# Column-grouped sums of squares, a table for low-rank products, a re-planned instruction order and a divided last multiply in a hybrid RWKV-7 / DeltaNet layer

## The chip, the cores and the metric

The kernel runs on one core of a Trainium2 chip. The metric is the device time of one execution in microseconds, as the median of several runs: 2253.88 us over 3 runs (2250.65 to 2256.99) before the change. The engines are named as in the profile: PE is TensorE, and PEld its weight loads, DVE is VectorE, ACT is ScalarE, POOL is GpSimd, SP is SyncE, which issues most of the DMAs.

## The reference

One layer over 256 latent tokens and 256 context tokens, width D = 2048, all in float32. Cut to what matters:

```python
mod = silu(c) @ w_ada + b_ada                      # six vectors of D: shifts, scales, gates
h  = rmsnorm(x, norm1_w)   * (1 + sc1)  + sh1      # and hc from ctx with its own vectors
rw, cv, z, ab, gt = split(h @ w_in)                # one input projection
o_a = two-way RWKV-7 scan over 16 heads of 64      # low-rank decay, rate and gate inputs
o_b = two-way chunked gated DeltaNet, 8 heads of 128
    # u = silu(conv(cv)); q, k = l2norm(q), l2norm(k); v
m = sigmoid(g_a) * (o_a @ p_a) + sigmoid(g_b) * (o_b @ p_b)
x = x + gt1 * (m @ w_out)
x = x + gt2 * (silu(h2 @ w_gate) * (h2 @ w_up)) @ w_down
return rmsnorm(x, final_norm_w)
```

`rmsnorm(x, w)` is `x * rsqrt(mean(x * x) + 1e-6) * w`. The context states start the latent scans; only the latent output is returned.

## The kernel before

Features lie on the 128 partitions (16 tiles of D), tokens along the free axis: 256 latent and 256 context columns, 512 together. Every large product splits both operands in a high and a low part, and sums three products (hi·hi, lo·hi, hi·lo); a weight tile is loaded (`wraw`), cast on ACT (`whi`) and subtracted on DVE (`wlo`).

The kernel has four stages.

**First part** (lines 412 to 530, in program order by hand). The squares of x and of the context (ACT and DVE, line 447 and 448, two buffers `sq`) are summed over partitions by a product with a 128x128 matrix of ones (line 449), one for each of 16 tiles, all into one PSUM tile. A logarithm and an exponential give `rs`, the reciprocal root (lines 452 and 453). Then eight parts run, each for two tiles of D. A part loads four weight tiles `aw` of 1 MB (six buffers) and makes the modulation rows with narrow products, four column groups of 32 at a time (`ada_part`, line 461; four visits c = 0 to 3). `rows_of` (line 464) copies the rows, turns them on PE (line 469), and computes the modulated, normalised activations `hxh` and `hxl` of the two tiles. `low_products` (line 499) then adds this part's share to six accumulators: four groups of low-rank columns and the first key and receptance tile, in PSUM tiles `pi`, `mm`, `s`, `s`, `mm`, `pa`. It is a generator: one step is one accumulator, six products. These steps belong to the part before, and line 520 lays them between the visits of the present part: none after visit 0, one after visit 1, two after 2, one after 3, and the two left between the turn of the rows and their use. `low_split` (line 486) casts the low-rank weights, behind whose buffers on SP stand the next part's loads (`load_low`, `load_ada`).

**Woven stage** (`Weave`, lines 180 to 282). Some 20 kinds of generators yield operations for PE, DVE, ACT and POOL. A planner with a cost for each operation takes, again and again, the operation that could start first; where several could start at the same moment, the lowest rank wins (`RANK`, plus 10 for each pair or head). The order that comes out is fixed, engine by engine. The projection products (`products`, `cast`) have rank 900, so they fill PE where nothing else is ready; a gate column group has no reader in this stage, and `GATES_A` and `GATES_B` say after which pair (0 to 7) or head (0 to 7) how many of 40 may come. First come 8 pairs of RWKV heads (`prepare`, `grams`, `inverse`, `values`, `scan`), after the low-rank outputs (`lowrank`, `lowrank_out`), which ACT makes and stores to DRAM with DMAs of its own queue; then 8 DeltaNet heads (`features`, `tokens`, `decays`, `head_grams`, `head_inverse`, `head_scan`). In `features` ACT runs a Silu over 1280 columns, then a table load is planned, and `l2n` squares k on ACT, sums over partitions on PE with the ones and goes on with a logarithm on ACT and a multiply on DVE. In the planner a DMA that is issued on ACT or DVE costs 0.06 us (line 125), and Silu costs its elements alone.

**Merge, output projection, FFN, down projection** (lines 1515 to 1685), ordered by the framework.

**End** (lines 1686 to 1689). After the last residual add the squares, summed on the way, are summed over partitions; ACT takes the logarithm and the exponential (`rms_scale`, line 388), and DVE multiplies the 16 tiles by the scale in five pieces, each followed by its store on SP.

Rows of the profile for the woven stage all carry line 147, where operations are recorded, so they are told apart by tile names: `arena` holds many of them, `lo` are the low-rank outputs, `pa`, `pi`, `s`, `mm` are PSUM tiles.

Of the kernel before, what the change touches and what calls it, by code (L numbers as in the profile page):

```python
# [13 lines left out]
AF = mybir.ActivationFunctionType  # L14
# [4 lines left out]
P = 128  # L19
D = 2048  # L20
KT = D // P
T = 256
# [2 lines left out]
NPAIR = 8  # L25
NGH = 8
DECAY = 0.6065306597126334
GATES_A, GATES_B = (6, 2, 3, 4, 0, 1, 4, 3), (2, 2, 0, 1, 0, 1, 10, 1)

RANK = dict(cast=-94, lowrank=-64, prepare=59, grams=-6, inverse=-56, values=6, scan=-39, begin=181, head_scan=145, head_inverse=100, head_grams=123, decays=122, tokens=77, features=120, gate_out=137, lowrank_out=105, row_tile=486)  # L30
LAT = dict(dma=2.04, hop=0.255, own=0.092, grp=32, cg=4, turn=0.17)
LNEXP = "natural_log_exp_and_others"
SIGM = "sigmoid_and_others"
# [79 lines left out]
class Lane:  # L113
# [5 lines left out]
    def __getattr__(self, name):  # L119

        def op(out, *a, **k):
            if name == "preload_act_table_set":
                return Op(self, 1.3, lambda: self.engine.preload_act_table_set(out))
            if name == "dma_start":
                return Op(self, 0.6 if self.each > 0.0012 else 0.06, lambda: self.engine.dma_start(out, *a))
            n = int(np.prod(out.shape[1:]))
            kind = "full"
            if name == "transpose" and len(a) == 2:
                cost = 0.109
            elif name == "matmul":  # L130
                rows, m = a[0].shape[0], out.shape[0]
                if a[0].dtype == F32R:
                    cost, kind = 0.0035 + 0.000448 * n, "split"
                elif rows <= 64 and m <= 64:
                    cost, kind = (0.01 + 0.00037 * n if rows < 64 else 0.01 + 0.00075 * n), (rows, m)
                elif m <= 64:
                    cost, kind = 0.058 if m == 64 else 0.14, (rows, m)
                else:
                    cost = (0.0054 + 0.00167 * n) * (1.22 if rows == 96 else 1)
            else:  # L140
                psum = a and getattr(a[0], "tensor", None) is not None and "PSum" in type(a[0].tensor).__name__
                cost = (self.psum if psum else self.fixed) + self.each * n
                if name == "tensor_tensor_scan":
                    cost *= 1.9
                elif name == "scalar_tensor_tensor" and not psum:
                    cost *= 1.2
            return Op(self, cost, lambda: getattr(self.engine, name)(out, *a, **k), kind)  # L147
        return op


def quad(ops):
# [127 lines left out]
def emit(ctx: ExitStack, tc, A, out, dbg=None):  # L279
    nc = tc.nc  # L280
    V, S, G, Q = nc.vector, nc.scalar, nc.gpsimd, nc.sync
    E = nc.tensor
# [3 lines left out]
    e, v, s = Lane(E, 0.0, 0.0, 0.0), Lane(V, 0.07, 0.00104, LAT["own"], 0.13), Lane(S, 0.09, 0.00086, LAT["own"], 0.165)  # L286
# [6 lines left out]
    pa = ent(tc.tile_pool(name="pa", bufs=2, space=PSUM))  # L293
    pi = ent(tc.tile_pool(name="pi", bufs=1, space=PSUM))
    psq = ent(tc.tile_pool(name="psq", bufs=2, space=PSUM))
# [16 lines left out]
    ident, ones, bd64 = c_("ident"), c_("ones"), c_("bd64")  # L312
# [6 lines left out]
    eps, gneps = c_("eps"), c_("gneps")  # L319
# [3 lines left out]
    def pst(pool, tag, shape=None):  # L323
        return pool.tile([P, 512], F32, tag=tag, name=tag)
# [60 lines left out]
    H2 = (hx.tile([P, KT, 2, T], F32R, name="hxh"), hx.tile([P, KT, 2, T], F32R, name="hxl"))  # L385
    HX = tuple(t.rearrange("p k a t -> p k (a t)") for t in H2)

    def rms_scale(pool, parts, n, name):

        ps = pst(pa, "pa")  # L390
        for i, sq in enumerate(parts):
            E.matmul(ps[:, :n], ones, sq, start=i == 0, stop=i == len(parts) - 1)
        r = pool.tile([P, n], F32, tag=name, name=name)
        S.activation(r, ps[:, :n], AF.Ln, bias=eps, scale=1.0 / D)
        S.activation(r, r, AF.Exp, scale=-0.5)
        return r

    def square_sum(pool, src, acc, first):

# [12 lines left out]
    with tc.tile_pool(name="p0", bufs=1) as p0, \  # L412
# [31 lines left out]
        ps = pst(pa, "pa")  # L444
        for k in range(KT):
            sq = p0.tile([P, 2, T], F32, tag="sq", name="sq", bufs=2)
            S.activation(sq[:, 0], xt[:, k, :], AF.Square)
            V.tensor_mul(sq[:, 1], ct[:, k, :], ct[:, k, :])
            E.matmul(ps, ones, sq.rearrange("p a t -> p (a t)"), start=k == 0, stop=k == KT - 1)
        rs = p0.tile([P, 2, T], F32, name="rs")  # L450
        S.preload_act_table_set(LNEXP)
        S.activation(rs.rearrange("p a t -> p (a t)"), ps, AF.Ln, bias=eps, scale=1.0 / D)
        S.activation(rs, rs, AF.Exp, scale=-0.5)
        s1 = p0.tile([P, 2, 16], F32, name="s1")

# [43 lines left out]
        def low_products(e, w):  # L499

            for ps, (o, m, n) in zip(low, LOWS):
# [2 lines left out]
                         e == 0 and k == 0, e == NE - 1 and k == 1)  # L504
                yield

        before = None
        for part in range(NE + 1):
            if part < NE:
                ps = pst(pmm, "mm")  # L510
            for c in range(4):
                if part + 1 < NE:
                    load_ada(part + 1, c)
                if part < NE:
                    ada_part(ps, part, c)
                if c == 0 and part < NE:
                    w = low_split(part)
                    if part + 1 < NE:
                        load_low(part + 1)
                for _ in itertools.islice(before or (), (0, 1, 2, 1)[c]):  # L520
                    pass
            if part < NE:
                rows_of(part, ps, before or ())
                before = low_products(part, w)
            else:
                for _ in before:
                    pass
# [162 lines left out]
    rs = rk_ctx.enter_context(tc.tile_pool(name="rs", bufs=1, reuse_waits="tile"))  # L690
# [5 lines left out]
    rs = Places(rs, arena, *rplaces)  # L696
# [30 lines left out]
    def lowrank():  # L727
# [17 lines left out]
        for p in range(NPAIR):  # L745
# [8 lines left out]
            for j in (0, 2, 1, 3):  # L754
                ps = yield psb
                yield e.matmul(ps, w[:96, 4 * (p % 2) + j], lin[:, j], start=True, stop=True)
                weave.add(RANK['lowrank_out'], lowrank_out(p, j, ps, out[j]))

    def prepare(p):
# [78 lines left out]
        if p + 1 < NPAIR:  # L838
            weave.add(10 * p + 10 + RANK['prepare'], prepare(p + 1))

# [222 lines left out]
    def products():  # L1063
# [24 lines left out]
        while todo or nxt:  # L1088
            if nxt is None:
# [4 lines left out]
                if nxt[0] == "g":  # L1094
                    nxt = "g", next(gate_next)
                weave.add(RANK['cast'], cast(source(*nxt), i))
            what, p = nxt
            nxt = choose()
            if nxt is not None:
                if nxt[0] == "g":  # L1100
                    nxt = "g", next(gate_next)
                weave.add(RANK['cast'], cast(source(*nxt), i + 1))
            ps = yield mmb
# [10 lines left out]
            if what == "g":  # L1114
                weave.add(RANK['gate_out'], gate_out(rs, p, ps))
            else:
# [127 lines left out]
    def features(h):  # L1244

        o = hd[h]
        yield ("scalars",)
        if h:
            yield "feat", h - 1
        if h > 1:  # L1250
            for n in ("tok", "gram"):
                yield n, h - 2
        kvq = gs.tile([P, 1280], F32, tag="kvq", name="kvq")
        o["k"], o["v"], o["q"] = k, vv, q = kvq[:, 0:512], kvq[:, 512:1024], kvq[:, 1024:1280]
        for what, j, t, n in (("K", 8 + h, k, 2), ("V", 16 + h, vv, 2), ("Q", h, q, 1)):
            yield what + "gemm", h
            yield from conv(o[what + "ps"], j, t, n)
        yield s.activation(kvq, kvq, AF.Silu)
        yield s.preload_act_table_set(LNEXP)
        yield from l2n(k, 512)  # L1260
        yield from l2n(q, T, float(P) ** -0.5)
        weave.ready("feat", h)
# [185 lines left out]
    def ada_rest():  # L1448
# [23 lines left out]
        for i in range(4 * KT):  # L1472
            if i > 2:
                yield "added", i - 3
            if i % 8 == 0 and i:
                yield "gscan", i // 8 - 1
            weave.add(RANK['row_tile'], row_tile(i))
            if i % KT == KT - 1:
# [85 lines left out]
    for j in range(KT):  # L1564
        if j == 8:
            wpool.append(more)
        ps = pst(pmm, "mm")
# [6 lines left out]
    x1p = Places(None, arena, ("x1", KT * T, 1), ("rs", T, 1), ("ssum", T, 1), ("graw", 64, 1), ("s2", 16, 1), ("pad", 176, 1),  # L1574
                 ("cb", 2048, 1), ("sq", T, 3), ("m", T, 2), ("hb", T, 2))
    x1 = x1p.tile([P, KT, T], F32, name="x1")
    ssum = x1p.tile([P, T], F32, name="ssum")
# [7 lines left out]
    for j in range(KT):  # L1585
        ps = pst(pmm, "mm")
# [13 lines left out]
    for j in range(KT):  # L1600
        ps = pst(pmm, "mm")
        gemm(ps[:, 0:T], load_w(A["wout"][j], P, KT), M, T)
        V.scalar_tensor_tensor(x1[:, j, :], ps[:, 0:T], mod[:, 32 + j:33 + j], x1[:, j, :], ALU.mult, ALU.add)
        sq = square_sum(x1p, x1[:, j, :], ssum, j == 0)
# [9 lines left out]
        elif j % 3 == 2 and j < 12:  # L1614
            hi, lo = (W4[:, i, j // 3] for i in range(2))
            for c in range(2):
                k, raw = slice(8 * c, 8 * c + 8), coming.pop(0)
# [3 lines left out]
    r = rms_scale(x1p, [ssum, sq], T, "rs")  # L1621
# [6 lines left out]
    with tc.tile_pool(name="fp", bufs=1, reuse_waits="tile") as fp:  # L1628
# [19 lines left out]
        for j in range(NH):  # L1648
            if j < 2:
                ps = p4[j]  # L1650
            else:
                ps = pst(pmm, "mm")
# [8 lines left out]
            if 2 <= j < 34:  # L1661

                for a in range(2):
                    c = (j - 2) // 2
# [10 lines left out]
        for j in range(KT):  # L1675
            ps = pst(pmm, "mm")
# [5 lines left out]
            sq = square_sum(x1p, x1[:, j, :], ssum, j == 0)  # L1682
            if 0 < j < KT - 1:
                V.tensor_add(ssum, ssum, sq)
            S.activation(x1[:, j, :], x1[:, j, :], AF.Identity, scale=p_("nf", j))
        r = rms_scale(x1p, [ssum, sq], T, "rs")
        for k0, k1 in ((0, 4), (4, 8), (8, 12), (12, 14), (14, 16)):
            V.tensor_mul(x1[:, k0:k1], x1[:, k0:k1], r.unsqueeze(1).to_broadcast([P, k1 - k0, T]))  # L1688
            Q.dma_start(out[:, k0:k1, :], x1[:, k0:k1, :])


# [94 lines left out]
```

## Time and profile before

| what | us |
|---|---|
| median of 3 runs | 2253.88 |
| the profiled execution | 2266.56 |
| its span, first to last instruction | 2264.7 |
| PE busy | 2166.1 |
| DVE busy | 1562.9 |
| ACT busy | 1063.7 |
| mean granted clock of PE | 0.982 |

A line of a profile that stands for a group of instructions gives line, engine, operation, what is written and what is read, the count, the busy time and the mean in ns, and then the idle time of the engine just before, with what ended it. In a timeline a row starts with its start and its length in us, and the idle time before it stands in brackets with what released it. A row of waits gives the waiting engine with its tile and line, who ended the wait, total us, times and the longest. A row of windows gives the stretch, its length, the busy time of PE, weight loads, DVE, ACT and POOL with their counts, the clock of PE that was granted (1.00 is full), the busy share of the DMA engines, and GB/s. The strip lines cut the span into 40 slices of about 57 us, with tenths as digits.

### The profile page before, as it was taken

To read this page: it belongs to the slowest core of one execution; us is meant where nothing else is said; L and a number is where in the kernel's file an instruction comes from. 1 tells how busy PE (TensorE), PEld (TensorE's weight loads), DVE (VectorE), ACT (ScalarE), POOL (GpSimd) and SP (SyncE) were. 2 spreads that over 40 slices of the span, in tenths; PEclk is the share of its full clock that TensorE was granted. 3 is DMA by queue.
4 is the path that set the end of the run, shared out by engine and by line. 5 is a ranking of instruction groups with operands and counts; after the bars stand their busy time and mean duration, and the time that the engine had idled before them with its cause. 6 is when DMAs were issued, how large, how long until landed. Compare 5 with 4: busy or idle time off the path is not lost. (4 is left out here: it accounts for less than half of the span.)

```text
span 2264.7 us, 54396 instructions
## 1 busy us (share of the span) xinstructions
PE 2166.1 (96%) x22778; PEld 1925.6 (85%) x22778; DVE 1562.9 (69%) x3253; ACT 1063.7 (47%) x1878; POOL 91.3 (4%) x169
## 2 busy tenths in 40 slices
PE   7998999999999999999999989999999999999998
PEld 4776588777778778877788989989999999999997
DVE  3456388778888668899898878865666665444544
ACT  3245555444554555454455554544444444444443
POOL 0000000000000010111110010000000000000000
PEclk9998999999999999999999999999999999999999
DMA  9955644344344346565558798845777776566665
GB/s 380 408 138 165 184 121 134 98 111 107 99 121 113 115 133 185 162 183 172 173 171 250 249 325 271 310 145 176 234 234 233 235 238 210 187 187 187 188 191 161
DMA packets 234485, 435.14 MB, mean 192 GB/s; under 512 B 115328, under 2 KB 129664, under 8 KB 229888
## 3 DMA queue, kind: packets, MB, share of 16 engines
q1 hardware_dynamic: 206304, 355.11, 50.5%
q0 software_dynamic: 14112, 51.39, 7.1%
q10 hardware_dynamic: 13824, 25.17, 3.3%
q8 instruction: 179, 2.93, 0.6%
q14 instruction: 66, 0.54, 0.1%
HBM read 405.76 MB, written 25.84 MB: 191 GB/s over the span
## 5 line engine op out<-in xcount | busy, mean ns | idle before, releaser
L364 DVE TENSOR_TENSOR wlo<-wraw,whi 128x1024 fp32r<-128x1024 f32 x328 | 392.7, 1198 | 331.6 <-ACT whi L363 329.3
L363 ACT CAST whi<-wraw 128x1024 fp32r<-128x1024 f32 x328 | 337.2, 1028 | 474.8 <-PE mm L374 377.4
L147 PE MATMUL mm<-hxh,whi 128*128 128x256 f32 (+1 forms) x1376 | 465.6, 338 | 7.7 <-ACT whi L147 7.5
L147 PE MATMUL mm<-hxh,wlo 128*128 128x256 f32 (+1 forms) x1376 | 466.5, 339 | 4.4 <-DVE wlo L147 4.3
L147 PE MATMUL mm<-hxl,whi 128*128 128x256 f32 (+1 forms) x1376 | 463.7, 337 | 0.0
L375 PE MATMUL mm<-hfh,wlo 128*128 128x256 f32 x1344 | 375.5, 279 | 0.4 <-DVE wlo L364 0.2
L374 PE MATMUL mm<-hfl,whi 128*128 128x256 f32 x1344 | 375.2, 279 | 0.0
L373 PE MATMUL mm<-hfh,whi 128*128 128x256 f32 x1344 | 375.2, 279 | 0.0
L147 PEld LDWEIGHTS mm<-hxh,whi 128*128 128x128 f32 x1376 | 265.0, 193 | 34.4 <-ACT whi L147 9.2
L147 PEld LDWEIGHTS mm<-hxh,wlo 128*128 128x128 f32 x1376 | 264.7, 192 | 30.9 <-DVE wlo L147 8.2
L147 PEld LDWEIGHTS mm<-hxl,whi 128*128 128x128 f32 x1376 | 264.7, 192 | 24.2 <-issue 3.0
L147 DVE TENSOR_TENSOR wlo<-wraw,whi 128x512 fp32r<-128x512 f32 x344 | 235.4, 686 | 68.4 <-ACT whi L147 65.5
L375 PEld LDWEIGHTS mm<-hfh,wlo 128*128 128x128 f32 x1344 | 252.7, 188 | 0.8 <-DVE wlo L364 0.8
L373 PEld LDWEIGHTS mm<-hfh,whi 128*128 128x128 f32 x1344 | 252.7, 188 | 0.0
L374 PEld LDWEIGHTS mm<-hfl,whi 128*128 128x128 f32 x1344 | 252.7, 188 | 0.0
L147 ACT CAST whi<-wraw 128x512 fp32r<-128x512 f32 x344 | 205.8, 617 | 95.3 <-PE mm L147 65.7
L147 DVE TENSOR_TENSOR arena<-arena 128x28 f32<-128x28 f32 (+13 forms) x538 | 131.2, 246 | 22.5 <-DMA arena<-scr 9.1
L373 PE MATMUL mm<-za,whi 128*128 128x256 f32 x512 | 143.0, 279 | 0.0
L375 PE MATMUL mm<-za,wlo 128*128 128x256 f32 x512 | 142.9, 279 | 0.0
L374 PE MATMUL mm<-za,whi 128*128 128x256 f32 x512 | 142.8, 279 | 0.0
L147 ACT ACTIVATE arena<-arena 128x512 f32<-128x512 f32 (+3 forms) x132 | 76.7, 592 | 48.5 <-DVE arena L147 35.7
L373 PEld LDWEIGHTS mm<-za,whi 128*128 128x128 f32 x512 | 96.2, 188 | 0.0
(320 smaller groups left out, 3911.7 us busy)
## 6 DMA issues: line engine op xcount, KB each, us to landing
wraw<-w SPq DMA_DIRECT2D x172, 512.0 KB, 4.1
wraw<-wgu SPq DMA_DIRECT2D x168, 512.0 KB, 4.6
aw<-ada_rest POOLq DMA_DIRECT2D x96, 512.0 KB, 5.4
aw<-ada_first SPq DMA_DIRECT2D x32, 1024.0 KB, 11.6
wraw<-wdn SPq DMA_DIRECT2D x64, 448.0 KB, 3.7
wraw<-wout SPq DMA_DIRECT2D x32, 512.0 KB, 5.7
aw<-ada_gt ACTq DMA_DIRECT2D x64, 256.0 KB, 4.9
wraw<-wdn SPq DMA_DIRECT2D x32, 512.0 KB, 3.6
```

Source lines behind the costliest of these rows:

```text
L147: return Op(self, cost, lambda: getattr(self.engine, name)(out, *a, **k), kind)
L363: S.copy(hi[:, c, :M], raw[:, c, :M])
L364: V.tensor_sub(lo[:, c, :M], raw[:, c, :M], hi[:, c, :M].bitcast(F32))
L373: E.matmul(ps, hi, Xh[:, k, :n], start=first and i == 0, stop=False)
L374: E.matmul(ps, hi, Xl[:, k, :n], start=False, stop=False)
L375: E.matmul(ps, lo, Xh[:, k, :n], start=False, stop=last and i == len(wt) - 1)
```

## The change

Four edits.

- **Squares.** Each product with ones uses 32 columns and writes one quarter of the PSUM tile's partitions, quarter k mod 4, so that four tiles' sums stand in four quarters. DVE copies the tile, and one more full product with ones adds the 128 rows, in which each quarter's sum stands 32 times; the scale is divided by 32.
- **Table.** `TILES[part][c]` says how many low-rank steps follow visit c, part by part.
- **Plan.** Two costs of the planner: a DMA issued on ACT is 0.33 us instead of 0.06, and Silu in `features` costs 1.3 us more (`slow`). No instruction is added by these. The ranks of `grams`, `begin` and `decays` change, and one gate group moves from pair 3 to head 5. The order of the woven stage comes out anew.
- **Last products.** `rms_scale` can also write the exponential to a PSUM tile, ahead of the one to SBUF. DVE multiplies 11 tiles by the copy in PSUM, POOL multiplies 5 tiles by the one in SBUF; the five stores stay on SP, in the order of the loop.

```diff
-GATES_A, GATES_B = (6, 2, 3, 4, 0, 1, 4, 3), (2, 2, 0, 1, 0, 1, 10, 1)
+GATES_A, GATES_B = (6, 2, 3, 3, 0, 1, 4, 3), (2, 2, 0, 1, 0, 2, 10, 1)
-RANK = dict(..., grams=-6, ..., begin=181, ..., decays=122, ...)
+RANK = dict(..., grams=34, ..., begin=196, ..., decays=137, ...)
...
-                return Op(self, 0.6 if self.each > 0.0012 else 0.06, lambda: self.engine.dma_start(out, *a))
+                return Op(self, 0.6 if self.each > 0.0012 else 0.33, lambda: self.engine.dma_start(out, *a))
...
+def slow(op):
+    op.cost += 1.3
+    return op
...
-    def rms_scale(pool, parts, n, name):
+    def rms_scale(pool, parts, n, name, keep=False):
...
         S.activation(r, ps[:, :n], AF.Ln, bias=eps, scale=1.0 / D)
+        if keep:
+            two = pst(psq, "s")
+            S.activation(two[:, :n], r, AF.Exp, scale=-0.5)
         S.activation(r, r, AF.Exp, scale=-0.5)
-        return r
+        return (two[:, :n], r) if keep else r
...
-            E.matmul(ps, ones, sq.rearrange("p a t -> p (a t)"), start=k == 0, stop=k == KT - 1)
+            quarter = slice(32 * (k % 4), 32 * (k % 4) + 32)
+            E.matmul(ps[quarter], ones[:, 0:32], sq.rearrange("p a t -> p (a t)"), start=k < 4, stop=k >= KT - 4)
...
-        S.activation(rs.rearrange("p a t -> p (a t)"), ps, AF.Ln, bias=eps, scale=1.0 / D)
+        V.tensor_copy(rs.rearrange("p a t -> p (a t)"), ps)
+        ps = pst(pa, "pa")
+        E.matmul(ps, ones, rs.rearrange("p a t -> p (a t)"), start=True, stop=True)
+        S.activation(rs.rearrange("p a t -> p (a t)"), ps, AF.Ln, bias=eps, scale=1.0 / (32 * D))
...
+        TILES = ((0, 0, 0, 0), (1, 1, 1, 1), (1, 1, 1, 1), (0, 2, 1, 1), (0, 1, 2, 1),
+                 (0, 2, 1, 1), (0, 1, 2, 1), (0, 1, 1, 1), (0, 2, 1, 1))
...
-                for _ in itertools.islice(before or (), (0, 1, 2, 1)[c]):
+                for _ in itertools.islice(before or (), TILES[part][c]):
...
-        yield s.activation(kvq, kvq, AF.Silu)
+        yield slow(s.activation(kvq, kvq, AF.Silu))
...
-        r = rms_scale(x1p, [ssum, sq], T, "rs")
-        for k0, k1 in ((0, 4), (4, 8), (8, 12), (12, 14), (14, 16)):
-            V.tensor_mul(x1[:, k0:k1], x1[:, k0:k1], r.unsqueeze(1).to_broadcast([P, k1 - k0, T]))
+        r = rms_scale(x1p, [ssum, sq], T, "rs", keep=True)
+        for en, by, k0, k1 in ((V, 0, 0, 4), (G, 1, 11, 13), (V, 0, 4, 8), (G, 1, 13, 16), (V, 0, 8, 11)):
+            en.tensor_mul(x1[:, k0:k1], x1[:, k0:k1], r[by].unsqueeze(1).to_broadcast([P, k1 - k0, T]))
             Q.dma_start(out[:, k0:k1, :], x1[:, k0:k1, :])
```

More of the change, by code (lines that the diff above doesn't have):

```diff
@@ L27 @@
 DECAY = 0.6065306597126334
-GATES_A, GATES_B = (6, 2, 3, 4, 0, 1, 4, 3), (2, 2, 0, 1, 0, 1, 10, 1)
-RANK = dict(cast=-94, lowrank=-64, prepare=59, grams=-6, inverse=-56, values=6, scan=-39, begin=181, head_scan=145, head_inverse=100, head_grams=123, decays=122, tokens=77, features=120, gate_out=137, lowrank_out=105, row_tile=486)
+GATES_A, GATES_B = (6, 2, 3, 3, 0, 1, 4, 3), (2, 2, 0, 1, 0, 2, 10, 1)
+RANK = dict(cast=-94, lowrank=-64, prepare=59, grams=34, inverse=-56, values=6, scan=-39, begin=196, head_scan=145, head_inverse=100, head_grams=123, decays=137, tokens=77, features=120, gate_out=137, lowrank_out=105, row_tile=486)
 LAT = dict(dma=2.04, hop=0.255, own=0.092, grp=32, cg=4, turn=0.17)
```

## The prediction

> **What bounds the kernel now.** I read the page first: which engine is full, and in which slices. Then the busy time by stage, the waits of the stages that the change touches, and the instructions in order of time around those waits.
>
> ```profile
> PE 2166.1 (96%) x22778; PEld 1925.6 (85%) x22778; DVE 1562.9 (69%) x3253; ACT 1063.7 (47%) x1878; POOL 91.3 (4%) x169
> ...
> DMA  9955644344344346565558798845777776566665
> ```
>
> ```profile
> 133.00:1288.00 1155.00, 1103.49 (x13450) 904.47 (x13449) 926.54 (x2315) 594.89 (x1252) 72.44 (x130) 0.97 0.51 150
> ...
> 1288.00:1510.00 222.00, 202.85 (x1644) 195.74 (x1642) 170.59 (x246) 112.08 (x156) 18.50 (x34) 0.98 0.84 288
> 1510.00:2254.00 744.00, 742.75 (x6338) 741.99 (x6338) 406.73 (x541) 318.18 (x399) 0.00 (x0) 1.00 0.65 200
> ```
>
> TensorE is the bound nearly everywhere (columns: length, then busy us of PE, weight loads, DVE, ACT, POOL, then clock and DMA share). The FFN and the down projection, 1510 to 2254, leave it 1 us idle; no edit is there, so a gain made earlier passes straight through. The woven stage, 133 to 1288, leaves PE idle for 1155.0 - 1103.5 = 51.5 us, and its mean clock of 0.97 costs up to 0.03 x 1155 = 35 us more. The first part is both DMA and PE, since the DMA line begins with 99. So a gain must come from PE's waits ahead of 133, from the 51.5 us, or from the tail after 2254.
>
> **The change part by part.** The sum is made against the profiled execution: 2266.56 us, span 2264.7. That is 12.7 above the median of the three runs, 2253.88, so I subtract the sum from the median. A measurement of this kernel can tell about 0.3%, 6.8 us.
>
> *Squares on four column groups.*
>
> ```profile
> 21.18 0.42 ACT L447 ACTIVATE sq<-xt 128x256 f32<-128x256 f32 x1 [0.44 <-PE pa L449]
> ...
> 27.20 0.69 ACT L452 ACTIVATE rs<-pa,C 128x512 f32<-128x512 f32 x1
> ...
> 29.03 0.81 ACT L494 CAST whi<-wraw 128x736 fp32r<-128x736 f32 x1 [0.48 <-DMA wraw<-w_low]
> ```
>
> ```profile
> 29.87 1.89 DVE L495 TENSOR_TENSOR wlo<-wraw,whi 128x736 fp32r<-128x736 f32 x2 [3.97 <-ACT whi L494]
> 31.67 0.28 DVE L467 COPY rows<-mm 128x128 f32<-128x128 f32 x1
> ```
>
> ```profile
> 27.08 3.70 PE L461 MATMUL mm<-aw,ckr 128*32 128x128 f32 x128
> ```
>
> A square now comes every 0.42 + 0.44 = 0.86 us, the time of one product. Four column groups let products overlap, but the squares sit in two buffers: the third must wait for the first product (0.86), be squared (0.42) and be handed over twice (29.03 + 0.81 to 29.87 is 0.03; I allow 0.1), 1.5 us for two, 0.75 each. Sixteen save about 0.11 x 16 = 1.8. Added: a PSUM copy of 128x512 on DVE (nearest row, ACT's read of that tile: 0.69), one full product (0.86) and two handovers, 1.8. The new product waits for that copy, and behind it on PE stand the 128 instructions of part 0's modulation rows. Net 0, or +1.8 if nothing overlaps. Cover: DVE copies the rows only at 31.67, behind the wlo subtractions, which wait for ACT and that for the w_low DMA at 29.03. The rows' products end at 27.08 + 3.70 = 30.78, so a gain here is worth nothing and 0.9 us of a loss is covered; 0.9 is the worst. I take 0.
>
> *Table of low-rank products.*
>
> ```profile
> 32.51 1.08 PE L461 MATMUL mm<-aw,ckr 128*32 128x128 f32 x32 [0.17 <-DMA aw<-ada_first]
> 37.37 1.94 PE L461 MATMUL mm<-aw,ckr 128*32 128x128 f32 x32 [3.78 <-DMA aw<-ada_first]
> 39.23 0.80 PE L373 MATMUL pi<-hxh,whi 128*128 128x512 f32 x1
> 42.09 1.38 PE L461 MATMUL mm<-aw,ckr 128*32 128x128 f32 x32
> ...
> 46.40 1.08 PE L461 MATMUL mm<-aw,ckr 128*32 128x128 f32 x32
> ```
>
> ```profile
> 35.69 0.48 DVE L483 SCALAR_TENSOR_TENSOR hxl<-ct,modc,hxh 128x256 fp32r<-128x256 f32 x1
> ```
>
> ```profile
> 35.50:42.30 6.80, 4.93 (x42) 3.43 (x46) 2.34 (x4) 1.03 (x2) 0.00 (x0) 0.53 1.01 413
> ```
>
> ```profile
> L427 SPq DMA_DIRECT2D aw<-ada_first x3: 378/431/1166, 31.2 to 33.0; - x3
> ...
> DMA to landing us min/median/max: 6.1/8.1/9.6
> ```
>
> In part 1 PE waits 3.78 us for its second weight tile, then runs at clock 0.53 until 42.3. The table puts the six pi products ahead of that wait. Their last operand is there at 35.69 + 0.48 = 36.2, so they fill the hole and end near 37.5. Today they lie at 39.23 to 42.09, 2.86 us. The next two tiles land by 33.0 + 9.6 = 42.6, while PE uses them at 42.09 and 46.40: it can run about 3 us earlier here. SP's loads wait only for buffers that free earlier. The limit is the DMA:
>
> ```profile
> L427 SPq DMA_DIRECT2D aw<-ada_first x1: 424/424/424, 66.5 to 66.5; - x1
> ...
> DMA to landing us min/median/max: 8.3/8.3/8.3
> ```
>
> ```profile
> 75.74 1.95 PE L461 MATMUL mm<-aw,ckr 128*32 128x128 f32 x64
> ```
>
> This tile lands at 74.8 and is used halfway through that group, 76.7: 1.9 us of slack on DMA engines whose share is already 1.01. So the lead is 1.9 to 3.2; I take 2.5. A separate visit costs 2 x 1.08 - 1.95 = 0.2 more than a joined one, in parts 1 and 2, inside that slack. In part 7 one product group more goes behind the transpose, where PE now waits:
>
> ```profile
> 125.92 0.50 PE L374 MATMUL pi<-hxl,whi 128*128 128x512 f32 x1 [0.54 <-DVE hxl L483]
> ```
>
> That is -0.5. Bounds for the table: -3.7 to 0, taken -3.0.
>
> *The Silu estimate.* `slow` changes no instruction, only the planned time.
>
> ```profile
> 1072.43 1.28 ACT L147 ACT_TABLE_LOAD   x1 [0.37 <-DVE arena L147]
> 1073.72 1.27 ACT L147 ACTIVATE arena<-arena 128x1280 f32<-128x1280 f32 x1
> 1075.01 1.28 ACT L123 ACT_TABLE_LOAD   x1
> ```
>
> ```profile
> PE pa L147 <- ACT arena L147: 7.9, 8, 1.7
> ```
>
> ```profile
> 1077.51 2.07 PE L147 MATMUL pa<-arena,C 128*128 128x512 f32 x2 [1.68 <-ACT arena L147]
> ```
>
> ```profile
> 1020.00:1076.00 56.00, 53.09 (x551) 44.66 (x550) 50.09 (x131) 27.10 (x54) 5.89 (x9) 1.00 0.59 169
> ```
>
> ```profile
> 1076.60:1080.00 3.40, 2.49 (x4) 1.36 (x5) 3.04 (x8) 1.75 (x4) 0.02 (x1) 0.56 0.75 258
> ```
>
> The plan counts the load after Silu, not the 1.28 us before it, so the norm's product stands 1.28 too early in PE's fixed order. PE waits there once in each of eight heads, 7.9 us in all, with projection products queued behind it that could have run. The longest, 1.68, is followed by 3.4 us at clock 0.56: another 1.5. Corrected, projection products go first, and what is late next is the Ln on ACT that reads the norm's sum, which PE need not wait for. But DVE has 50.09 of 56 us in such a head, so I count 70%: -5.5 and -1.0. By the Trainium skill, "TensorE: Matmul & The Clock Gate", Part 1, the clock falls only after an idle window of about 3.4 us; none of the waits quoted here is that long, so the gain would be 1.0 smaller. The row at 1076.60 disagrees, and the row decides.
>
> *The DMA estimate.* ACT issues 32 stores of the low-rank outputs, planned 0.06 us each:
>
> ```profile
> 164.14 0.69 ACT L147 ACTIVATE lo<-s,PR 128x512 f32<-128x512 f32 x1
> ...
> 164.85 0.35 ACTq L125 DMA_DIRECT2D sgd__1344<-lo  x1
> 165.25 0.69 ACT L147 ACTIVATE lo<-s,PR 128x512 f32<-128x512 f32 x1
> ```
>
> ```profile
> 135.53 0.39 PE L147 MATMUL mm<-hxh,whi 128*128 128x256 f32 x1 [1.85 <-ACT whi L147]
> ```
>
> ```profile
> PE mm L147 <- ACT whi L147: 6.2, 4, 2.0
> PE s L147 <- ACT lo L147: 3.2, 4, 1.6
> ```
>
> ACT cannot start the next output before the issue ends. It falls 32 x 0.27 = 8.6 us behind its plan between 164 and 260; casts that feed PE queue behind it. PE's waits on ACT from 133 to 300 are 9.4 us. The one at 135.53 comes before any of these stores; of the other 7.5 I count 40%, -3.0, with bounds 0 and -7.5: the buffers of `lo` and the table loads stay.
>
> *Ranks and gates.* No instruction is added. One gate group moves from pair 3 to head 5, with its casts. The ranks decide only between pieces that could start at the same moment, but a greedy order drifts from there. No row prices this. The nearest are one hole and the half-clock stretch after it, 1.68 + 1.5 = 3.2 us; two or three of these either way give -8 to +8. I take 0.
>
> *Divided last products.*
>
> ```profile
> 2255.88 4.70 DVE L1688 TENSOR_TENSOR arena<-arena 128x1024 f32<-128x1024 f32 x5 [2.19 <-ACT arena L395]
> ```
>
> ```profile
> 2260.00:2262.00 2.00, 0.00 (x0) 0.00 (x0) 0.58 (x1) 0.00 (x0) 0.00 (x0) 0.50 0.99 392
> ```
>
> ```profile
> L147 POOL TENSOR_TENSOR arena<-arena,gct 128x512 f32<-128x512 f32 x16 | 18.4, 1149 | 153.6 <-DMA arena<-grow 79.7 <-DVE gct L147 48.9 <-DVE PT L147 24.9
> ```
>
> DVE has 11 rows of 16, 4.70 x 11/16 = 3.2, and ends near 2259.1. POOL starts one Exp later, about 2256.3, and needs 1.15 for two rows and 1.7 for three, to 2259.2. All is ready 1.4 us sooner. But the 2.1 MB of output, at the 392 GB/s of that row, take 5.4 us at a DMA share of 0.99, and the first store still follows the first DVE product. The gain is hidden: 0. Bounds: -0.1 (0.01 of 5.4 us is all the share leaves), and +1.2, if POOL has to wait for one DVE product of four rows (4.70 / 4), since DVE's later stores stand on SP behind POOL's.
>
> Sum: 0 - 3.0 - 6.5 - 3.0 + 0 + 0 = -12.5: 2254.1 for a profiled run, 2241.4 as a median.
>
> **The rivals.**
> 1. *DVE takes over in the heads.* For it: 50.09 of 56 us, and the moved gate group brings DVE casts into head 5. Against: DVE still idles 6 us per head, more than the 1 us asked for. Then only the table and a little of the ACT term remain, -3 to -5: about 2250, no change that can be told. Chance 0.20.
> 2. *Slower: the new order opens holes in PE.* Place: pairs 1 to 7 and heads, where a late cast or Gram product leaves PE in its fixed order. Each costs 3.2 us as above. Four more of these than now cancel the gain, six reach the bound of slower, seven give -12.5 + 22.4 = +9.9: 2263.8. Against: the two errors that the plan is cleared of are the ones that the trace shows. Chance 0.12.
> 3. *Larger gain.* The mean clock of 0.97 stands for up to 35 / 1.5 = 23 half-clock stretches. If shorter waits take five of them along, -12.5 - 7.5 = -20.0: 2233.9. Against: most of PE's waits stay. Chance 0.13.
>
> That squares and tail do nothing, though they do what they say, is in the forecast as two zeros.
>
> **How the numbers follow.** The forecast, 2241.4, has 0.55. Faster by over 0.3% is the forecast and rival 3: 0.68. Rival 1 is 0.20, rival 2 0.12. The range runs from 2231, 3 below rival 3, to 2257, which is rival 1 with most of the order's +8 on it; outside lie rival 2 and a little of rival 3.
>
> **What would show it.** Right: PE's wait for the second weight tile near 37 us falls under 1.5 us and the woven stage starts 2 to 4 us earlier; PE's wait on ACT ahead of the norm products falls from 7.9 to under 3 us; PE's idle time in the woven stage falls to about 43; the DMA share after the first output store stays near 1 and the time from the last DVE residual add to the end is unchanged within 0.5 us. Wrong: the norm waits vanish but the woven stage is no shorter, with DVE fuller in each head (rival 1); or more stretches at half clock than now (rival 2).

## The result, and the profile after

The changed kernel takes 2243.32 us as the median of 8 runs (2237.13 to 2244.57), the kernel before 2257.59 on the same chip (8 runs, 2250.65 to 2266.29). The ratio is 0.9929, with a 95% interval of 0.9909 to 0.9949, about 16 us; the medians themselves differ by 14.3 us. The profiled execution of the changed kernel took 2240.53, its span is 2238.8. The spans of the two profiled executions differ by 25.9 us, more than either says: the one of before (2266.56) lies above all eight of its runs, the one of the changed kernel below its median. So traces are used to see where a stage changed, and sizes are taken from the ratios.

The first lines of the page after, to be laid beside those of before:

```profile
PE 2158.4 (96%) x22780; PEld 1918.6 (86%) x22780; DVE 1556.9 (70%) x3252; ACT 1062.9 (47%) x1879; POOL 94.6 (4%) x171
...
DMA  9955544344344446465667887836777776566665
```

PE is still the bound, and its idle time in the span fell from 2264.7 - 2166.1 = 98.6 to 2238.8 - 2158.4 = 80.4 us. Where it fell is seen if both traces are cut at the same three points: the first product of the woven stage, the end of the last projection product (`mm<-hxh,wlo` of line 147), and the first FFN activations `hfh`. Windows of before (length, then PE, weight loads, DVE, ACT, POOL, clock, DMA share, GB/s):

```profile
0.00:135.50 135.50, 117.02 (x1352) 83.55 (x1352) 55.38 (x150) 38.84 (x74) 0.52 (x6) 0.97 0.94 351
135.50:1287.60 1152.10, 1102.45 (x13442) 903.68 (x13442) 925.11 (x2312) 592.71 (x1248) 72.32 (x129) 0.97 0.51 150
1287.60:1510.30 222.70, 203.47 (x1647) 196.31 (x1647) 171.26 (x248) 112.78 (x157) 18.50 (x34) 0.98 0.84 288
1510.30:2264.70 754.40, 743.19 (x6340) 742.03 (x6339) 411.15 (x546) 319.41 (x402) 0.00 (x0) 0.99 0.65 200
```

And the same four stretches after:

```profile
0.00:131.00 131.00, 113.14 (x1354) 78.39 (x1354) 55.41 (x151) 38.22 (x74) 0.52 (x6) 1.00 0.96 363
131.00:1263.80 1132.80, 1098.31 (x13442) 901.49 (x13442) 921.23 (x2312) 591.79 (x1249) 72.58 (x129) 0.97 0.52 153
1263.80:1484.20 220.40, 203.76 (x1647) 196.85 (x1647) 171.02 (x249) 112.87 (x157) 18.49 (x34) 0.98 0.84 291
1484.20:2238.70 754.50, 743.17 (x6340) 741.89 (x6339) 409.28 (x544) 319.96 (x402) 3.03 (x2) 0.99 0.64 200
```

The first part is 4.5 us shorter, the woven stage 19.3, the stretch after it 2.3, and the rest is 0.1 us longer. In the woven stage the number of products is the same, 13442; PE's idle time went from 49.7 to 34.5 us, and its mean clock stayed at 0.97.

Two views show the steps that the prediction named. In time, PE in part 1 after:

```profile
33.34 0.50 PE L378 MATMUL pi<-hxh,whi 128*128 128x512 f32 x1 [0.79 <-ACT hxh L493]
34.38 0.50 PE L379 MATMUL pi<-hxl,whi 128*128 128x512 f32 x1 [0.54 <-DVE hxl L495]
...
36.53 1.08 PE L473 MATMUL mm<-aw,ckr 128*32 128x128 f32 x32 [0.62 <-DMA aw<-ada_first]
```

```profile
35.50:42.30 6.80, 5.74 (x82) 3.78 (x84) 1.28 (x2) 0.00 (x0) 0.00 (x0) 1.00 1.00 416
```

The `pi` products stand ahead of the second weight tile, PE waits 0.62 us for it instead of 3.78, and the stretch that ran at clock 0.53 runs at 1.00. Among PE's waits from 128 to 1264 (total, times, longest), the largest are now:

```profile
PE pi L147 <- DVE arena L147: 6.1, 9, 1.5
PE mm L147 <- ACT whi L147: 5.8, 4, 1.9
PE mm L147 <- DVE wlo L147: 4.7, 7, 1.7
PE pi L147 <- issue: 4.2, 3, 2.1
...
PE s L147 <- ACT lo L147: 1.9, 4, 1.2
```

The wait of the norm product on ACT (`PE pa <- ACT arena`), 7.9 us in eight places before, has left the heads.

### The profile page after: what moved, and what is told of

Read it like the earlier page. It is cut to its first block, busy times and chain, and to the rows that moved or that the text cites. A ratio compares the mean times of both kernels' runs of the same rounds, so it can differ in the third digit from the quotient of the medians.

```text
span 2238.8 us, 54403 instructions
## 1 busy us (share of the span) xinstructions
PE 2158.4 (96%) x22780; PEld 1918.6 (86%) x22780; DVE 1556.9 (70%) x3252; ACT 1062.9 (47%) x1879; POOL 94.6 (4%) x171
## 4 chain that ended last, share of the span: by engine, by line
issue 40%; PE 38%; DVE 9%; DMA 9%; ACT 2%; POOL 0%; SPq 0%; POOLq 0%; ACTq 0%; DVEq 0%
PE mm L147 22%; PE s L147 5%; PE pa L147 4%; DVE arena L147 3%; PE pi L147 3%; DVE wlo L147 1%; DMA wraw<-wout 1%; DMA aw<-ada_first 1%; DVE wlo L369 1%; PE mm L473 1%; PE mm L380 1%; DMA wraw<-pb 1%; PE mm L378 1%; PE mm L379 1%; DMA wr<-wgu 1%
```

## The experiments

All are edits of the kernel before. Their medians stand beside runs of before on the same chip. In the texts on parts of the change the theory is that of the prediction: the terms add up, one by one. For the order of the woven stage its rival is that the order gains only as a whole, the estimates together with the ranks and the gate group that go with them.

**The Silu estimate alone.**

```diff
+def slow(op):
+    op.cost += 1.3
+    return op
...
-        yield s.activation(kvq, kvq, AF.Silu)
+        yield slow(s.activation(kvq, kvq, AF.Silu))
```

> The kernel before with the Silu estimate alone. Theory (named waits): PE's waits on ACT ahead of the norm products fall from 7.9 us to under 3 us, the DeltaNet stage (first-head store of the last pair to the first merge product, 456 us before) gets 5 to 9 us shorter, the whole 6.5 us, a ratio near 0.997. Rival A (DVE bound): the waits go, the stage stays within 2 us of 456, with DVE busier by its share. Rival B (only the redrawn order counts): the waits go, but the stage moves by an amount that has nothing to do with 7.9, up to 8 us either way.

Measured: 2269.18 against 2262.52, ratio 1.0033 (1.0018 to 1.0049): slower, where the theory wanted a gain. The trace shows where the gain was lost. The two windows run from the last pair's end (its last addition on DVE, `Y<-Y,bon`) to the last projection product, and from there to the first `hfh`. Before:

```profile
836.40:1287.60 451.20, 429.48 (x4629) 372.98 (x4628) 397.88 (x1021) 222.13 (x441) 47.81 (x74) 0.99 0.63 190
```

and from there 222.7, as shown above. With the Silu estimate alone:

```profile
832.50:1275.40 442.90, 425.66 (x4567) 369.70 (x4565) 392.18 (x1014) 219.50 (x436) 46.96 (x73) 1.00 0.63 191
1275.40:1512.30 236.90, 212.26 (x1710) 204.87 (x1710) 176.15 (x258) 117.08 (x164) 19.00 (x35) 0.95 0.80 275
```

The heads are 8.3 us shorter, as the theory had it and against rival A, and the norm waits are nearly gone:

```profile
PE pa L147 <- ACT arena L147: 1.1, 2, 0.8
```

But the stretch behind is 14.2 longer. 63 products more stand in it (1710 against 1647), PE is idle there for 24.6 us instead of 19.2, and its clock is 0.95 instead of 0.98. So 5.4 of the 14.2 us are idle time; the other 8.8 are busy time, and most of that goes with the lower clock (0.05 of 236.9 us against 0.02 of 222.7, about 7 us by this rough estimate). The products in time say which these are. In before, the large step of the last head's inverse (64x64, written to `pi`) stands just ahead of the last projection product:

```profile
1277.71 0.45 PE L147 MATMUL pi<-Tx,qo 32*32 32x32 f32 x32
...
1286.54 0.68 PE L147 MATMUL pi<-Tx,arena 64*64 64x64 f32 x16 [1.18 <-DVE arena L147]
...
1287.37 0.28 PE L147 MATMUL mm<-hxh,wlo 128*128 128x256 f32 x1
```

With the Silu estimate alone the projections end first, and the last head is still in its inverse:

```profile
1274.54 0.45 PE L147 MATMUL pi<-Tx,qo 32*32 32x32 f32 x32 [0.93 <-DVE qo L147]
...
1275.14 0.27 PE L147 MATMUL mm<-hxh,wlo 128*128 128x256 f32 x1
1277.14 0.51 PE L378 MATMUL mm<-oah,whi 128*128 128x256 f32 x2 [1.72 <-ACT oah L383]
1279.26 0.58 PE L379 MATMUL mm<-oal,whi 128*128 128x256 f32 x1 [1.61 <-DVE oal L384]
...
1282.12 0.45 PE L147 MATMUL pi<-qo,Tx 32*32 32x32 f32 x32
...
1287.02 0.68 PE L147 MATMUL pi<-T,LT 64*64 64x64 f32 x16 [1.54 <-ACT T L147]
...
1292.60 0.68 PE L147 MATMUL pi<-Tx,arena 64*64 64x64 f32 x16
```

The step comes 17.5 us after the last projection product instead of 0.8 before it. Counted from the last pair's end, the projections end 8.3 us earlier, and this step comes 10.0 us later (460.1 instead of 450.1). The chain had not come forward with the projections: its earlier step `pi<-Tx,qo` stands at 442.0 us, against 441.3 in before. From there to the large step it takes 18.1 us instead of 8.8. The eight waits were filled with projection products, and their supply is fixed: from the last pair's end on, 1866 of them run here and 1864 in before. Behind `pi<-Tx,qo` of head 7 there are 2 left, where before has 50. The serial chain of head 7 was left with the merge products alone. In PE's fixed order the first of these stand ahead of the chain's next step (`pi<-qo,Tx`, 1282.12), and PE has to wait for their operands (`oah`, `oal`).

**The DMA estimate alone.**

```diff
-                return Op(self, 0.6 if self.each > 0.0012 else 0.06, lambda: self.engine.dma_start(out, *a))
+                return Op(self, 0.6 if self.each > 0.0012 else 0.33, lambda: self.engine.dma_start(out, *a))
```

> The kernel before with the DMA estimate alone. Theory: the low-rank stage (end of the first part to the last low-rank output, 127.7 us before) gets 3 us shorter, PE's waits there on ACT fall from 9.4 to about 6.5 us, the norm waits in the heads stay near 8 us; whole: -3 us, ratio 0.9987. Rival B: the low-rank stage is the same and what changes lies elsewhere.

Measured: 2261.52, ratio 0.9990 (0.9974 to 1.0006). That is -2.3 us, between -5.9 and +1.4: the -3.0 of the prediction is inside, and so is a change of 0. In this trace PE still waits 3.8 us on `lo` (3.2 before), and with the 5.4 us on `whi` that makes 9.2, where 6.5 was expected: the named waits hardly shrank. From the first woven product to the start of the last `lo` it takes 124.5 us, 125.9 in before.

```profile
PE s L147 <- ACT lo L147: 3.8, 5, 1.6
```

**Ranks and gate group alone,** with the old estimates.

```diff
-GATES_A, GATES_B = (6, 2, 3, 4, 0, 1, 4, 3), (2, 2, 0, 1, 0, 1, 10, 1)
+GATES_A, GATES_B = (6, 2, 3, 3, 0, 1, 4, 3), (2, 2, 0, 1, 0, 2, 10, 1)
-RANK = dict(..., grams=-6, ..., begin=181, ..., decays=122, ...)
+RANK = dict(..., grams=34, ..., begin=196, ..., decays=137, ...)
```

> The kernel before with the three ranks and the moved gate group alone, with the old estimates. Theory: no gain, within 3 us of before, and the norm waits stay near 8 us. Rival B (order): 5 us or more of the 14 are here, in the DeltaNet stage.

Measured: 2263.10 against 2262.52, ratio 1.0009 (0.9995 to 1.0023). Alone they gain nothing, and the norm waits of the heads stay, 7.4 us.

**Both estimates, old ranks and gates.**

> The kernel before with both corrected estimates, with the old ranks and gates. Theory (named waits): the two gains add, -9.5 us, ratio 0.996. Rival B (order): less than half of that, as the ranks and gates that belong to the corrected plan are not there.

Measured: 2262.90 against 2262.43, ratio 0.9998 (0.9981 to 1.0015). From the last pair's end to the last projection product, and on to `hfh`:

```profile
828.10:1269.00 440.90, 426.17 (x4568) 370.79 (x4566) 391.57 (x1014) 219.70 (x436) 46.09 (x73) 0.99 0.63 192
1269.00:1500.70 231.70, 207.30 (x1710) 199.97 (x1710) 176.07 (x258) 116.37 (x164) 19.02 (x35) 0.97 0.82 281
```

10.3 us are saved in the heads, 9.0 are given back behind them, with the same 1710 products there. The last head's large step is late again, 16.2 us after the last projection product.

**The whole plan:** both estimates, the ranks and the gate group; squares, table and end as before.

> The kernel before with the whole plan edit: both estimates, ranks and gates. Theory: the same as with the estimates alone within 3 us, so -9 to -12 us, ratio 0.995 to 0.996. Rival B: clearly better than the estimates alone, by 5 us or more.

Measured: 2250.75 against 2262.43, ratio 0.9942 (0.9922 to 0.9963), about 13 us faster. The same two windows:

```profile
831.70:1271.20 439.50, 426.32 (x4631) 372.70 (x4629) 394.38 (x1024) 221.93 (x443) 48.14 (x74) 0.99 0.64 195
1271.20:1487.60 216.40, 201.08 (x1647) 193.95 (x1647) 172.00 (x249) 112.36 (x157) 18.51 (x34) 1.00 0.85 296
```

The gain in the heads is there (11.7 us), and nothing is given back: 1647 products stand behind the last projection product, as in before. The 6.3 us by which this stretch is shorter than in before go with a clock of 1.00 instead of 0.98; this trace, at 2243.06, is one of the faster runs of its kernel.

So the theory that the terms add up falls, and the rival stands so far only as a total. From the traces I formed a sharper one, A in the next text: the Silu estimate pays in the heads, on condition that projection products are left for head 7; the gate group at head 5 and the rank of `decays` are that condition.

**The Silu estimate with cover for the last head.** As the first experiment, with

```diff
-GATES_A, GATES_B = (6, 2, 3, 4, 0, 1, 4, 3), (2, 2, 0, 1, 0, 1, 10, 1)
+GATES_A, GATES_B = (6, 2, 3, 3, 0, 1, 4, 3), (2, 2, 0, 1, 0, 2, 10, 1)
-RANK = dict(..., decays=122, ...)
+RANK = dict(..., decays=137, ...)
```

> The Silu estimate as in e1_silu, with one gate group moved from pair 3 to head 5 and the rank of `decays` raised from 122 to 137; the DMA estimate, the other two ranks, squares, table and end as before. Theory A (the estimate pays in the heads, and loses it where the last head has no projection products left beside it; gate group and `decays` give it that cover): from the last pair's end to the last projection product 443 us, as in e1_silu (442.9; before 451.2); from there to the first FFN product 222, as before (222.7), and not 237 as in e1_silu; so 8 us faster, ratio 0.9965, between 0.995 and 0.998. Theory B (the whole of the planned order, with the DMA estimate and the other two ranks in it, is what gains, and no place can be named): the ratio stays above 0.9985, as with the estimates alone (0.9998) or the ranks and the gate group alone (1.0009), or the 8 us in the heads are gone.

Measured: 2251.70 against 2262.43, ratio 0.9959 (0.9943 to 0.9976), about 9 us faster: inside what A gave (its two lengths, 443 and 222, came out at 439.4 and 220.2), and outside B's. The windows and the products in time:

```profile
832.10:1271.50 439.40, 426.16 (x4632) 372.49 (x4630) 394.05 (x1024) 221.91 (x443) 47.85 (x74) 0.99 0.64 195
1271.50:1491.70 220.20, 203.68 (x1646) 196.78 (x1647) 171.10 (x249) 112.77 (x156) 18.50 (x34) 0.98 0.84 291
```

```profile
1270.34 0.68 PE L147 MATMUL pi<-Tx,arena 64*64 64x64 f32 x16 [0.80 <-DVE arena L147]
1271.18 0.28 PE L147 MATMUL mm<-hxh,wlo 128*128 128x256 f32 x1
```

The last head's step stands 0.8 us ahead of the last projection product again, and the stretch behind it takes 220.2 us. Counted from the last pair's end the step comes at 438.2 us, against 450.1 in before and 460.1 with the Silu estimate alone: here the chain came forward too, by 12 us. The supply is the same 1866 projection products. It is spent otherwise than with the Silu estimate alone: from `pi<-Tx,qo` of head 1 to that of head 2 there are 180 instead of 239, from head 3 to head 4 there are 151 instead of 179, and behind that of head 7 there are 50 left. Against the Silu estimate alone, one gate group and one rank turn 1.0033 into 0.9959, 16.7 us. Gate group and `decays` were not run apart from each other, so which of them does how much is open.

**The table alone.**

```diff
+        TILES = ((0, 0, 0, 0), (1, 1, 1, 1), (1, 1, 1, 1), (0, 2, 1, 1), (0, 1, 2, 1),
+                 (0, 2, 1, 1), (0, 1, 2, 1), (0, 1, 1, 1), (0, 2, 1, 1))
...
-                for _ in itertools.islice(before or (), (0, 1, 2, 1)[c]):
+                for _ in itertools.islice(before or (), TILES[part][c]):
```

> The kernel before with the table of low-rank products alone. Theory: the wait for the second weight tile near 37 us falls from 3.8 to under 1.5 us, no half clock follows it, and the first part ends 3 to 3.5 us earlier (133.7 before); whole -3 us, ratio 0.9987. Rival (DMA bound): the wait goes, but PE waits for later tiles instead, and the first part ends less than 1.5 us earlier.

Measured: 2259.83 against 2262.52, ratio 0.9982 (0.9966 to 0.9999), about 4 us. The woven stage begins at 131.97. In the runs without the table whose first square product comes at nearly the same time (9.6 to 9.8 us) it begins at 134.45 (ranks alone) and 134.71 (DMA estimate alone), so the table moved it by 2.5 to 2.7 us, a little less than the 3 to 3.5 expected and well over the rival's 1.5. PE waits 0.36 us for the second weight tile. The expectation that no half clock follows did not hold here: a wait of 1.68 us stands ahead of the first weight tile of this part, and five of the six `pi` products behind it still take 0.63 us each, where they take 0.39 to 0.50 in the trace of the whole change. With plan and table together, 0.9942 x 0.9982 = 0.9924; the whole change measured 0.9929.

**The squares alone,** and **the divided last products alone.** Their edits are the first and the last block of the diff above.

> The kernel before with the squares on four column groups alone. Theory: a square every 0.75 to 0.82 us instead of 0.86, but the first modulation rows are copied when the low-rank weights have been split, as before, so the first part ends within 0.7 us of before once the start of the loads is counted out; whole within 0.3%. Rival: the product over all rows delays the rows by 1 us or more.

Measured: 2260.05 against 2262.43, ratio 0.9993 (0.9976 to 1.0010). No change that can be told. From the first square product to the first woven product it takes 123.6 us, 124.6 in before: 1.0 where at most 0.7 was expected. The wait for the second weight tile is still there (3.62 us), but only the first of the `pi` products behind it run at half clock (0.63 us, then 0.39), so this 1.0 is not the squares' own.

> The kernel before with the divided last products alone. Theory (the output's DMA ends the kernel): the last product ends 1.2 to 1.5 us sooner after the residual add than before, and the time from the residual add's end to the end of the span stays at 11.0 us within 0.3. Rival: it falls by 1 us or more.

Measured: 2261.76 against 2262.43, ratio 0.9989 (0.9968 to 1.0010). No change either; the trace gives the place. DVE, POOL and the stores of SP at the end of this kernel:

```profile
2249.08 0.48 DVE L1684 SCALAR_TENSOR_TENSOR arena<-mm,mod,arena 128x256 f32<-128x256 f32 x1 [3.06 <-PE mm L375]
2251.73 3.22 DVE L1691 TENSOR_TENSOR arena<-arena,s 128x1024 f32<-128x1024 f32 x3 [2.16 <-ACT s L397]
2252.28 3.04 POOL L1691 TENSOR_TENSOR arena<-arena 128x512 f32<-128x512 f32 x2 [777.64 <-issue]
```

```profile
2254.58:2256.58 2.00, 0.00 (x0) 0.00 (x0) 0.36 (x1) 0.00 (x0) 0.75 (x1) 0.50 1.02 397
2256.58:2258.58 2.00, 0.00 (x0) 0.00 (x0) 0.00 (x0) 0.00 (x0) 0.00 (x0) 0.50 1.01 397
```

The products end at 2252.28 + 3.04 = 2255.3, 5.8 us after the residual add ends (2249.56); before it was 6.9, so they end 1.1 us sooner. But the DMA share is full from 2254.6 on, and the span ends 11.0 us after the add, as before (2264.7 - 2253.7).

**A quarter of the output stored,** once with undivided, once with divided products, to see the products without the stores that cover them.

```diff
-            Q.dma_start(out[:, k0:k1, :], x1[:, k0:k1, :])
+            Q.dma_start(out[:, k0:k1, 0:64], x1[:, k0:k1, 0:64])
```

> The kernel before, storing only the first 64 of 256 token columns of each tile, so three quarters of the output are left out. Theory (the output's DMA ends the kernel): with a quarter of the bytes the products are the bound, and from the end of the last residual add to the end of the span it takes 10 to 10.7 us instead of 11.0. Rival (a fixed latency after the last store ends it): 11.0 as before.

> The divided last products with the same quarter of the output stored. Theory: without the DMA's bound the earlier products pay, and the tail is 1 us or more shorter than with the undivided ones and the same quarter. Rival: the two tails are the same.

Each ran once. Undivided, the last residual add and the end of the span (2257.5) are 9.6 us apart; divided (2263.5), 8.8:

```profile
2247.40 0.48 DVE L1681 SCALAR_TENSOR_TENSOR arena<-mm,mod,arena 128x256 f32<-128x256 f32 x1 [3.06 <-PE mm L375]
```

```profile
2254.24 0.48 DVE L1684 SCALAR_TENSOR_TENSOR arena<-mm,mod,arena 128x256 f32<-128x256 f32 x1 [3.06 <-PE mm L375]
```

With little to store the division is worth 0.8 us, a little less than the 1 expected; with all of it, 0.0. That is the cover that the prediction named, by one run of each kernel. The undivided end became 1.4 us shorter (0.3 to 1.0 expected), so it is not a fixed latency after the last store that sets the 11.0. The total times, 2259.33 and 2265.47, differ by what happens far ahead of the end and say nothing about it.

**The kernel before once more.**

> The kernel before, unchanged, for a second profile. Theory: the profiled execution of before was some 9 us above its median by chance of its waits and half-clock stretches, so that this one lies between 2250 and 2262 us and its waits ahead of the norm products are again near 8 us. Rival: it is near 2266 us again and the profile adds the time.

Measured: 2267.09, with a span of 2265.3. I had expected it lower. So a profiled execution of before at 2265 is not a single stray: the runs of this one kernel spread over 15 us (2250.65 to 2266.29 in the result above), and no size of the whole is taken from one of them. That the profile adds the time is not borne out: the profiled executions of the changed kernel (2240.53) and of the whole plan (2243.06) lie below their medians.

## Why the prediction was right, and where its steps were not

The time, 2241.4 against 2243.32, and the side were right. That the time fits so closely is in part luck: the sum started from a median of 2253.88 for before, which beside the changed kernel was 2257.59; the change was forecast at -12.5 and measured at 14 to 16 us. That the parts add up is luck as well, since two of them are wrong in opposite ways. The parts:

- *Squares, 0: right.* A pair of squares now comes every 1.63 us (18.07, 19.70 and so on in the trace after), 0.815 each where 0.86 was before and 0.75 was expected. The added copy and product use that up and a little more: from the first square product to the logarithm it takes 16.9 us, 16.3 before. The copy of the rows still stands right behind the `wlo` subtractions, 28.91 + 1.79 against 30.62: the cover held.
- *Table, -3.0: right.* 2.5 to 2.7 us in the traces, 4 by the ratio, with the wait as foretold; the half clock is gone in the trace of the whole change, not in that of the table alone. In the trace after, the woven stage begins 4.5 us earlier than in before (2 to 4 was written), but about 1 us of that was there with the first square product already (9.97 against 10.94).
- *Silu estimate, -5.5 and -1.0: the place was right, and as a term of its own it was wrong.* The norm waits went, and 8 us with them in the heads. The 1.0 for the half clock did not come: the mean clock of the woven stage is 0.97 before and after, one trace each. The Trainium skill, "TensorE: Matmul & The Clock Gate", Part 1, lets the clock fall only after an idle window of about 3.4 us, so that removing such short waits would leave it alone. The unchanged mean agrees with that. The stretches at half clock do not: no wait of PE in the woven stage of before is longer than 2.5 us, and yet the row at 1076.60 has 0.56. And alone the estimate makes the kernel 0.33% slower. The step that failed is "what is late next is the Ln on ACT that reads the norm's sum, which PE need not wait for". I looked for what is late next in the same head. What was late next was the chain of head 7, up to 400 us further on. Projection products that fill a wait are taken from a fixed supply.
- *Ranks and gates, 0: the step that failed with it.* "No row prices this" was true of each head, yet the last projection product and the last head's chain could have been read in the trace of before; they stand 0.8 us apart, with 50 projection products behind `pi<-Tx,qo`. The Silu estimate alone spends 62 more than before ahead of that step in head 0 (315 instead of 253), so the cover had little to give. Alone they measured 0 (1.0009), with the estimates 12.7 us (0.9998 to 0.9942). The whole plan was forecast at -9.5 and measured -13, its parts at -9.5 (estimates) and 0 (ranks and gate group); the estimates alone measured 0, and the ranks and gate group on top of them -13.
- *DMA estimate, -3.0: not settled.* Its own interval holds -3.0 and 0, and the waits that I counted hardly changed with it in its own trace. All traces together lean towards a gain: from the first woven product to the start of the last `lo` the four with this estimate take 119.0 to 124.5 us, the ten without it 121.9 to 126.3, and the two waits on ACT are 7.1 to 9.2 us against 9.1 to 10.3. The means of the stretch are 3.4 us apart, but the ranges overlap. On top of the Silu estimate it takes the ratio from 1.0033 to 0.9998, whose intervals just miss each other. What the whole plan has over the Silu estimate with cover, 0.9942 against 0.9959, lies inside the intervals, and two more ranks are in it.
- *End, 0: right,* for the reason given: from the last residual add to the end it is 11.1 us in the trace after, 11.0 before. POOL took 3.0 us for its five tiles, against 2.85.

Of the rivals, DVE did not take over: PE's waits of `pi` on DVE rose from 3.5 to 6.1 us in the woven stage while it became shorter. Half-clock stretches did not go along: the woven stage keeps 0.97. PE's idle time there fell to 34.5 us, further than the 43 that was written as a sign. The slower side did exist, though not as seven small holes: it was one place, the last head, and it shows in the experiment that leaves the gate group and the ranks out. The forecast had the right sum in part because the change brought the estimates together with what they need.

## What to carry to other kernels

In a fixed order in which filler covers waits, the filler is a budget. Before a wait is counted as gained, look at where the filler runs out and what serial chain stands there; the gain is real only if that chain moves forward as well. Edits to such a plan are tried together and apart, since each of two may be worth nothing or less without the other.

Work on the last products pays only if the stores behind them leave room: read the DMA share between the last product and the end first.

## What the runs showed of the hardware that was not expected

- Two kernels whose ACT and DVE orders are the same up to the last pairs (the DMA estimate alone, and both estimates) took 124.5 and 119.5 us from the first woven product to the start of the last `lo`, with granted clocks of 0.92 and 0.96 in windows that begin at 132. One trace can't settle less than about 5 us in that stage.
- The first square product came at 9.2 to 11.3 us in kernels with the same instructions there, and the woven stage's start moves with it (134.5 to 136.7 with the old squares and without the table).
- Products of 32 columns into different quarters of one PSUM tile do overlap: a pair took 1.35 us on PE. The second square of a pair is ready 0.33 us after the first (two of 0.42 us in 0.75), so 1.35 - 0.33 = 1.02 us is one product, and the second adds no more than it comes later. The 1.63 us from pair to pair are one product, one square (0.42) and the handovers between them, since there are two buffers; PE itself had time left. The Trainium skill, "TensorEngine Tiling (Array Packing)", section "Overview", names up to 4 times the speed for 32 columns. No run here has four operands ready at once, so this is not tested.
- With 64 of 256 columns stored, the output's packets have 246 bytes on average, and at a DMA share of 0.74 (undivided products, 2253.5 to 2255.5) they moved 154 GB/s; whole rows moved about 390 at 1.01. So the stores of a quarter are not four times as fast.
